# Layer norms of a transposed transformer block: the input multiplied in place by the reciprocal root, and ScalarE makes both modulated tiles and the residual from it

## The chip, the cores and the metric

The kernel runs on one core of a Trainium2 chip. The metric is device time in microseconds (us) per execution; before the change the median of three runs is 1629.13 us (1628.31 to 1630.39). Engines are named as in the profile: PE is TensorE, PEld its weight load, DVE is VectorE, ACT is ScalarE, POOL is GpSimd, SP is SyncE, which here starts the loads.

## The reference, cut to what matters

A model of two layers works on 256 tokens of a picture (`LAT`) and 256 tokens of context (`CTX`), each of width 1024. A layer is a half feed-forward (FFN), a mixer (grouped attention in layer 0, an mLSTM in layer 1) and a second half FFN. Each part is the same frame:

```python
def modulate(h, shift, scale):
    return h * (1.0 + scale) + shift

def post_norm(h, delta, g, b):
    return layer_norm(DEEPNORM_ALPHA * h + delta, g, b)

def half_ffn(h, shift, scale, gate, w_in, w_out, g, b):
    xm = modulate(h, shift, scale)
    a, u = jnp.split(xm @ w_in, 2, axis=-1)
    y = (jax.nn.silu(a) * u) @ w_out
    return post_norm(h, 0.5 * gate * y, g, b)
```

So a norm ends one part, and the modulated norm is the next part's input. In the kernel the two affine maps are folded: with z the input less its mean, and r the reciprocal root of the variance (one number per token), the next part's input is x = c·z·r + e, and what the next part's result is later added to is a·z·r + b. The coefficients a, b, c and e are one number per feature.

## The kernel before, in words

Activations lie transposed: `h` has 128 partitions, 8 chunks of 128 features, and 512 tokens in a row, tokens 0 to 255 `LAT` and 256 to 511 `CTX`. A coefficient per feature is thus one number per partition, which an ACT or DVE instruction takes from a 128x1 operand; r differs along a row, so it is spread over all partitions by a matmul with ones (L447, "the broadcast") into a PSUM tile `rb`.

Matmuls run at a fast rate with operands rounded to fp32r. To keep precision each operand is split in two tiles: a rounded one, `xh`, and the rest, `xl = x - xh`. A product is three matmuls: `xh` with the rounded weights, `xl` with the rounded weights, `xh` with the rest of the weights. Weights come from HBM in pieces of 128x1024 (`raw`, three buffers), ACT casts a piece (L225 CAST), DVE makes the rest (L230 TENSOR_TENSOR); seven finished pieces can wait.

`norm` (L443 to L546) is a generator. A table of letters at each place of use says after which matmul its next step is issued, so it is interleaved by hand with the matmuls of the FFN, of attention or of the mLSTM; its matmuls and a few statistics are pinned to that order. All other instructions go where a scheduler puts them, which at build time lists the instructions of each engine in one fixed order by its own estimates; at run time each engine works its list strictly in order. Its steps: mean (L447), eight times "subtract the mean, square" (L467 DVE, L474 ACT), variance (L447 with 128x1 results, sums by L484), the reciprocal root (L254 to L268, tiny DVE instructions), the broadcast, and eight times the **x stage** (L531 to L546), one per chunk:

- L540 DVE: x = z·c·rb, reading `rb` from PSUM
- L541 ACT: xh = x + e, rounded (bias from a 128x1 operand)
- L542 DVE: xl = (x + e) - xh
- L544 ACT, once per norm: copies `rb` to SBUF as `rs`, for the residual

The residual (L556 to L564) is put off: a list `later` holds the chunks, and the loops of the next part take two at a time: L563 DVE: z = z·a·rs, in the loops' order, and L564 ACT: z = z + b.

There are nine passes of `norm`, so 72 chunks. I name them by the time of their x stage in the profile: attention's input LAT (375 us) and CTX (400); the next FFN's LAT (555) and CTX (579); the next layer's first FFN LAT (904) and CTX (929); the mLSTM's LAT (1256) and CTX (1281, no residual is kept); the last FFN's LAT (1446), a raw norm: there the first units read z itself and are mended later (L580 to L586), and `rs` is needed for that. Residuals: 64.

In an FFN a unit is a pair of PSUM tiles (gate and up) of 128x256 for one group, 24 matmuls each. Six PSUM buffers (`mm`) hold three units; a unit's pair is free again when ACT has read the gate tile (L588, Silu) and DVE the up tile (L589). Attention: L941 to L943 are its input products, L986 and L998 to L1009 the query norm and rotation, L1036 to L1056 the softmax and the turned probabilities. L1541 and L1546, at the kernel's start, make the first part's input from the plain `h`: two ACT instructions per chunk, then a DVE subtraction.

Of the kernel before, what the change touches and what calls it, by code (L numbers as in the profile page):

```python
# [9 lines left out]
F32 = mybir.dt.float32  # L10
# [3 lines left out]
AF = mybir.ActivationFunctionType  # L14
ALU = mybir.AluOpType
# [3 lines left out]
P = 128  # L19
# [3 lines left out]
TL = 256  # L23
# [5 lines left out]
ALPHA = (2.0 * 2) ** 0.25  # L29
# [143 lines left out]
class Body:  # L173
# [23 lines left out]
    def mm(self):  # L197
        return self.t([P, 512], tag="mm", bufs=6, pool=self.pp)
# [227 lines left out]
    def pin(self, ins):  # L426

        return self.tc.keep_in_program_order(ins)
# [14 lines left out]
    def norm(self, g, coef, keep=True, nxt=True, alone=False):  # L443


        nc, V, S = self.nc, self.nc.vector, self.nc.scalar
        mm = lambda *k, **kw: self.pin(nc.tensor.matmul(*k, **kw))  # L447
        t0, t1 = g
        w = t1 - t0
        n = w // P  # L450
        raw = alone and nxt
        v = 0 if t0 == 0 else 1
# [11 lines left out]
        for d in range(ND):  # L464
            yield
            z = self.h[:, d, t0:t1]
            V.tensor_tensor(out=z, in0=z, in1=m[:, :w], op=ALU.subtract)  # L467
            if raw:
                c = coef()[1][:, v, d : d + 1]
                xh = self.xh[:, d, TL:T]  # L470
# [10 lines left out]
            else:  # L481
                a, s2 = sums[eng]
# [12 lines left out]
        x = self.small(n)  # L495
        pin = self.pin
        if most:
# [3 lines left out]
            for i in range(n):  # L501
                c = var[:, n + i : n + i + 1]
                V.tensor_scalar(c2[:, i : i + 1], c, c, -0.5, ALU.mult, ALU.mult)
            V.scalar_tensor_tensor(x, var[:, :n], 0.5 * LN_EPS, c2, ALU.add, ALU.add)
        else:
            V.tensor_scalar(x, var[:, :n], 0.5 * LN_EPS, None, ALU.add)

        r = self.rsqrt_half(x, n, pin)
        dg = self.tmp(w)
        pin(V.tensor_tensor(  # L510
            out=dg.rearrange("p (n f) -> p n f", n=n), in0=self.ident[:, None, :].broadcast_to([P, n, P]),
            in1=r[:, :, None].broadcast_to([P, n, P]), op=ALU.mult,
        ))
        if most:
# [3 lines left out]
            for d in range(ND):  # L518
                if eng[d] is not V:
                    z = self.h[:, d, t0:t1]  # L520
                    eng[d].tensor_tensor(out=z, in0=z, in1=dls, op=ALU.subtract)
        yield
        rb = self.ps()
        mm(rb[:, :w], self.ones, dg, start=True, stop=True)
        rs = self.t([P, TL], tag="rs", bufs=2) if keep and nxt else None
        if raw:
            S.copy(rs, rb[:, :w])
            dr = self.t([P, TL], tag="s1", bufs=S1B)
            V.scalar_tensor_tensor(dr, dls, -1.0, rs, ALU.mult, ALU.mult)
            self.raw_norm = rs, dr  # L530
        for d in range(ND):  # L531
            yield
            z = self.h[:, d, t0:t1]
            if most and eng[d] is V:
                V.tensor_tensor(out=z, in0=z, in1=dls, op=ALU.subtract)
            ab, c, e = coef()
            x = self.tmp(w)
            xh = self.xh[:, d, t0:t1]
            e = e[:, v, d : d + 1]
            V.scalar_tensor_tensor(x, z, c[:, v, d : d + 1], rb[:, :w], ALU.mult, ALU.mult)  # L540
            S.activation(xh, x, AF.Identity, bias=e)  # L541
            V.scalar_tensor_tensor(self.xl[:, d, t0:t1], x, e, xh.bitcast(F32), ALU.add, ALU.subtract)  # L542
            if d == 1 and rs is not None and not raw:
                S.copy(rs[:, :w], rb[:, :w])  # L544
            if keep:
                self.later.append((z, ab[:, 0, d : d + 1], ab[:, 1, d : d + 1], rs[:, :w]))  # L546

    def modulate(self, z, d, g, c, e, eng):
        t0, t1 = g
# [6 lines left out]
    def residual(self, n, pin=lambda ins: ins):  # L556

        for _ in range(min(n, len(self.later))):
            z, a, b, r = self.later.pop(0)
            if b is None:  # L560
                self.nc.scalar.activation(z, z, AF.Copy, scale=a)
            else:
                pin(self.nc.vector.scalar_tensor_tensor(z, z, a, r, ALU.mult, ALU.mult))  # L563
                self.nc.scalar.activation(z, z, AF.Identity, bias=b)  # L564


    def ffn_g(self, j, pa, pu, g, raw=False):
# [881 lines left out]
def start(b):  # L1449
# [4 lines left out]
    nc, pin = b.nc, b.pin  # L1454
    V, S = nc.vector, nc.scalar
# [73 lines left out]
    def modulated(d):  # L1529
        jobs = []  # L1530
        for v, g in enumerate((LAT, CTX)):
            z, x, xh = b.h[:, d, g[0] : g[1]], b.tmp(TL), b.xh[:, d, g[0] : g[1]]
            jobs.append((z, x, xh, ec[:, d, 0, v : v + 1], ec[:, d, 1, v : v + 1], b.xl[:, d, g[0] : g[1]]))
            b.later.append((z, ALPHA, None, None))
        for i in range(2):
            for v, (z, x, xh, e, c, _) in enumerate(jobs):
                o = x if i else xh
                if d == 0 and v and not i:
                    pin(V.tensor_scalar(o, z, c, e, ALU.mult, ALU.add))
                else:  # L1540
                    last = pin(S.activation(o, z, AF.Identity, bias=e, scale=c))  # L1541
        b.fence = {last.ins.engine: last} if d == ND - 1 else {}
        xs[d] = [(l, x, xh) for _, x, xh, _, _, l in jobs]
# [33 lines left out]
    first_by_pe()  # L1577
    cast(0)
    modulated(0)
    b.silu(pin)  # L1580
    low(ws[0][2], ws[0][0], ws[0][1])
    for d in range(ND):
# [22 lines left out]
        if n < ND:  # L1605
            modulated(n)
            low(ws[n][2], ws[n][0], ws[n][1])
# [161 lines left out]
```

## Time and profile before

| what | value |
|---|---|
| median of three runs | 1629.13 us |
| the profiled execution: its span | 1625.5 us |
| median less span | 3.6 us |
| PE busy | 1606.9 us, 99% |
| DVE busy | 1355.7 us, 83% |
| ACT busy | 749.2 us, 46% |
| POOL busy | 63.0 us, 4% |

The profile shows one execution. Its own time is the span and what lies around it (start and end); taken as 3.6 us here, the difference to the median. In rows of the timeline the first number is the start in us from the span's start, the second the time to the end of the last of the instructions grouped in the row, and "[0.68 <-ACT t L225]" says that the engine stood idle 0.68 us before it, until an ACT instruction of line 225 was done. Instructions of one engine overlap, so a group of n is shorter than n single ones.

### The profile page before, as it was taken

The page shows a single profiled execution, that of the slowest core. Times are in us where ns is not written, and L with a number is a line of the kernel's source. Part 1 is how long each engine was busy: PE and PEld are TensorE (multiplying, and loading weights), DVE is VectorE, ACT ScalarE, POOL GpSimd, SP SyncE. Part 2 cuts the span into 40 slices and gives each one's busy share as a digit, 9 for nine tenths or more (in the row PEclk, how much of TensorE's full clock was granted, in tenths as well). Part 3 has the DMA queues.
Part 4 walks back from the last instruction along what each step waited for, and adds up shares of the span by engine and source line. Part 5 has one row for each costly group of instructions (what it writes and reads, how often), then busy time and mean ns, then how long its engine had stood idle before and what let it go on. Part 6 is the DMA issues. An engine that isn't in the chain of part 4 may idle for free. (4 is left out here: it accounts for less than half of the span.)

```text
span 1625.5 us, 26587 instructions
## 1 busy us (share of the span) xinstructions
PE 1606.9 (99%) x10304; PEld 1451.7 (89%) x10304; DVE 1355.7 (83%) x2699; ACT 749.2 (46%) x1272; POOL 63.0 (4%) x77
## 2 busy tenths in 40 slices
PE   9999999999999999999999999999999999999998
PEld 7888888889988998889998998889999989999987
DVE  7899977649889879899986879699966968897687
ACT  6522132314676443316652444336652657566542
POOL 0000000001011100000000100000001000030000
PEclk9999999999999999999999999999999999999999
DMA  9687766422202447633445258713363343437552
GB/s 358 221 252 237 235 205 187 137 66 85 66 1 80 151 134 221 219 117 105 129 146 180 79 165 289 253 58 118 104 225 100 98 130 87 142 110 253 181 176 91
DMA packets 72222, 251.56 MB, mean 155 GB/s; under 512 B 7960, under 2 KB 10776, under 8 KB 72096
## 3 DMA queue, kind: packets, MB, share of 16 engines
q1 hardware_dynamic: 71520, 249.09, 47.7%
q8 instruction: 80, 1.31, 0.3%
q10 hardware_dynamic: 576, 0.79, 0.1%
q14 instruction: 46, 0.38, 0.1%
HBM read 248.79 MB, written 1.05 MB: 154 GB/s over the span
## 5 line engine op out<-in xcount | busy, mean ns | idle before, releaser
L241 PE MATMUL t<-t,t 128*128 128x256 f32 (+2 forms) x8412 | 1317.0, 318 | 6.4 <-ACT t L225 3.3
L241 PEld LDWEIGHTS t<-t,t 128*128 128x128 f32 x8412 | 1185.7, 188 | 125.4 <-ACT t L225 4.7
L225 ACT CAST t<-t 128x1024 fp32r<-128x1024 f32 (+3 forms) x521 | 428.5, 844 | 485.8 <-PE t L241 214.5
L230 DVE TENSOR_TENSOR t<-t,t 128x256 fp32r<-128x256 f32 (+2 forms) x740 | 513.8, 729 | 111.9 <-ACT t L225 107.7
L350 DVE SCALAR_TENSOR_TENSOR t<-t,t 128x1024 bf16<-128x1024 f32 x224 | 260.7, 1220 | 0.0
L588 ACT ACTIVATE t<-t 128x512 f32<-128x512 f32 (+1 forms) x71 | 34.5, 490 | 103.5 <-PE t L241 102.4
L941 PE MATMUL t<-t,t 128*128 128x256 f32 (+1 forms) x256 | 79.3, 310 | 0.0
L718 DVE SCALAR_TENSOR_TENSOR t<-t,t,t 128x256 f32<-128x256 f32 x96 | 42.7, 478 | 43.9 <-PE t L241 43.7
L943 PE MATMUL t<-t,t 128*128 128x256 f32 (+1 forms) x256 | 78.4, 306 | 0.0
L942 PE MATMUL t<-t,t 128*128 128x256 f32 (+1 forms) x256 | 78.4, 306 | 0.0
L589 DVE TENSOR_TENSOR t<-t,t 128x512 f32<-128x512 f32 (+1 forms) x71 | 39.0, 553 | 40.6 <-PE t L241 28.1
L484 POOL TENSOR_TENSOR t<-t,t 128x256 f32<-128x256 f32 x30 | 23.4, 781 | 1104.9 <-ACT t L474 1103.5
L869 PE MATMUL t<-t,t 128*128 128x512 f32 (+1 forms) x300 | 60.5, 364 | 0.0
L869 PEld LDWEIGHTS t<-t,t 128*128 128x128 f32 x300 | 51.5, 189 | 8.9
L474 ACT ACTIVATE t<-t 128x256 f32<-128x256 f32 x72 | 26.1, 412 | 65.5 <-DVE t L467 65.5
L1456 PE MATMUL t<-t,t 128*128 128x512 f32 (+2 forms) x276 | 55.6, 356 | 0.0
L1456 PEld LDWEIGHTS t<-t,t 128*128 128x128 f32 (+1 forms) x276 | 44.9, 183 | 10.9 <-issue 0.9
L942 PEld LDWEIGHTS t<-t,t 128*128 128x128 f32 x256 | 48.1, 188 | 3.0 <-DVE t L230 0.5
L941 PEld LDWEIGHTS t<-t,t 128*128 128x128 f32 x256 | 48.3, 189 | 2.7
L943 PEld LDWEIGHTS t<-t,t 128*128 128x128 f32 x256 | 48.1, 188 | 2.5
L541 ACT ACTIVATE t<-t,t 128x256 fp32r<-128x256 f32 x72 | 32.8, 503 | 30.1 <-DVE t L540 30.1
L641 DVE TENSOR_TENSOR t<-t,t 128x512 f32<-128x512 f32 x66 | 45.2, 685 | 0.4
(206 smaller groups left out, 1078.6 us busy)
## 6 DMA issues: line engine op xcount, KB each, us to landing
t<-in_ffn_in SPq DMA_DIRECT2D x168, 512.0 KB, 4.1
t<-in_ada_w SPq DMA_DIRECT2D x138, 512.0 KB, 4.4
t<-in_ffn_out SPq DMA_DIRECT2D x66, 512.0 KB, 4.5
t<-in_ffn_last SPq DMA_DIRECT2D x22, 512.0 KB, 3.5
t<-in_att_in SPq DMA_DIRECT2D x12, 512.0 KB, 3.5
t<-in_att_out SPq DMA_DIRECT2D x8, 512.0 KB, 3.6
t<-in_ml_qk SPq DMA_DIRECT2D x8, 512.0 KB, 3.6
t<-in_ml_v SPq DMA_DIRECT2D x8, 512.0 KB, 3.5
```

Of the source, the lines that this page charges most:

```text
L225: self.behind(self.nc.scalar.copy(h, x))
L230: self.behind(self.nc.vector.tensor_tensor(out=ls, in0=xs, in1=hs.bitcast(F32), op=ALU.subtract))
L241: mm = lambda *k, **kw: self.nc.tensor.matmul(*k, skip_group_check=not group, **kw)
L350: ins = nc.vector.scalar_tensor_tensor(self.tmp().bitcast(BF16), r, 1.0, self.cb[:, v, :], ALU.mult, ALU.mult, accum_out=to)
L589: V.tensor_tensor(out=sl, in0=sl, in1=pu[:, :n], op=ALU.mult)
L641: add = lambda o, x, y: V.tensor_tensor(out=o, in0=x, in1=y, op=ALU.add)
L718: V.scalar_tensor_tensor(z, y[:, gg[0] - t0 : gg[1] - t0], gate()[:, v, d : d + 1], z, ALU.mult, ALU.add)
L869: pin(nc.tensor.matmul(o, gs[g], ws[k][w][:, i : i + n], start=k == k0 and g == w == 0, stop=k == k1 - 1 and g == 1,))
L941: mm(o, self.xh[:, k, c], wh, start=k == 0, stop=False)
L942: mm(o, self.xh[:, k, c], wl, start=False, stop=False)
L943: mm(o, self.xl[:, k, c], wh, start=False, stop=k == ND - 1)
L1456: mm = lambda *k, **kw: pin(nc.tensor.matmul(*k, **kw))
```

## The change

In the x stage z is multiplied by `rb` in place (DVE, one TENSOR_TENSOR). ACT then makes xh = c·z + e and the plain x = c·z + e from it, two ACTIVATE instructions with scale and bias from 128x1 operands; DVE subtracts (TENSOR_TENSOR). Since z already holds the product with r, the residual is one ACT instruction a·z + b; its DVE part is gone, and with it `rs`, except in the raw norm, and the pin that held the residual to the loops' order.

```diff
-        rs = self.t([P, TL], tag="rs", bufs=2) if keep and nxt else None
         if raw:
+            rs = self.t([P, TL], tag="rs", bufs=1)
             S.copy(rs, rb[:, :w])
...
-            V.scalar_tensor_tensor(x, z, c[:, v, d : d + 1], rb[:, :w], ALU.mult, ALU.mult)
-            S.activation(xh, x, AF.Identity, bias=e)
-            V.scalar_tensor_tensor(self.xl[:, d, t0:t1], x, e, xh.bitcast(F32), ALU.add, ALU.subtract)
-            if d == 1 and rs is not None and not raw:
-                S.copy(rs[:, :w], rb[:, :w])
+            c = c[:, v, d : d + 1]
+            V.tensor_tensor(out=z, in0=z, in1=rb[:, :w], op=ALU.mult)
+            S.activation(xh, z, AF.Identity, bias=e, scale=c)
+            S.activation(x, z, AF.Identity, bias=e, scale=c)
+            V.tensor_tensor(out=self.xl[:, d, t0:t1], in0=x, in1=xh.bitcast(F32), op=ALU.subtract)
             if keep:
-                self.later.append((z, ab[:, 0, d : d + 1], ab[:, 1, d : d + 1], rs[:, :w]))
+                self.later.append((z, ab[:, 0, d : d + 1], ab[:, 1, d : d + 1]))
...
-                pin(self.nc.vector.scalar_tensor_tensor(z, z, a, r, ALU.mult, ALU.mult))
-                self.nc.scalar.activation(z, z, AF.Identity, bias=b)
+                self.nc.scalar.activation(z, z, AF.Identity, bias=b, scale=a)
```

New line numbers: the product in place is L541 (DVE), `xh` L542 and the plain x L543 (ACT), the subtraction L544 (DVE), the residual L563 (ACT). Lines behind it move up by one: Silu L588 becomes L587, its product L589 becomes L588.

Three places of the order, of before and of the change. First ACT's list at the end of the CTX x stage at 929 us; `t_67` is `xh`, `t_66` is `h` (z), `t_9331` in before and `t_9329` after the gate tile of the LAT unit ahead. Before:

```order
L541 ACTIVATE t_67<-t_9429,t_9030 128x256
L588 ACTIVATE t_9455<-t_9331 128x256
L541 ACTIVATE t_67<-t_9433,t_9030 128x256
L541 ACTIVATE t_67<-t_9437,t_9030 128x256
L225 CAST t_9453<-t_9455 128x256
L741 CAST t_9494<-t_67 128x256
L741 CAST t_9498<-t_67 128x256
L741 CAST t_9495<-t_68 128x256
L741 CAST t_9499<-t_68 128x256
L564 ACTIVATE t_66<-t_66,t_9023 128x256 x2
```

After the change:

```order
L542 ACTIVATE t_67<-t_66,t_9021,t_9017 128x256
L543 ACTIVATE t_9435<-t_66,t_9021,t_9017 128x256
L542 ACTIVATE t_67<-t_66,t_9021,t_9017 128x256
L543 ACTIVATE t_9440<-t_66,t_9021,t_9017 128x256
L587 ACTIVATE t_9459<-t_9329 128x256
L563 ACTIVATE t_66<-t_66,t_9014 128x256 x2
L225 CAST t_9457<-t_9459 128x256
L740 CAST t_9498<-t_67 128x256
L740 CAST t_9499<-t_68 128x256
```

The Silu (L588, now L587) that frees the gate tile stood between the stage's sixth and seventh L541; now it stands behind all sixteen activations of the stage, and the copies of `xh` and `xl` (L741, now L740) behind it and two residuals.

Second PE's list where attention's CTX products begin, at 405 us; `t_3469` is the first CTX tile in before and `t_3481` after, `t_3494` and `t_3506` the second. Rows from the sixth chunk on, before:

```order
L941 MATMUL t_3469<-t_3131,t_67 128x256
L942 MATMUL t_3469<-t_3131,t_67 128x256
L943 MATMUL t_3469<-t_3131,t_68 128x256
L941 MATMUL t_3469<-t_3131,t_67 128x256
L942 MATMUL t_3469<-t_3131,t_67 128x256
L943 MATMUL t_3469<-t_3131,t_68 128x256
L941 MATMUL t_3469<-t_3131,t_67 128x256
L942 MATMUL t_3469<-t_3131,t_67 128x256
L943 MATMUL t_3469<-t_3131,t_68 128x256
L941 MATMUL t_3494<-t_3111,t_67 128x256
```

After the change:

```order
L940 MATMUL t_3481<-t_3137,t_67 128x256
L941 MATMUL t_3481<-t_3137,t_67 128x256
L940 MATMUL t_3506<-t_3117,t_67 128x256
L941 MATMUL t_3506<-t_3117,t_67 128x256
L942 MATMUL t_3481<-t_3137,t_68 128x256
L940 MATMUL t_3481<-t_3137,t_67 128x256
L941 MATMUL t_3481<-t_3137,t_67 128x256
L942 MATMUL t_3506<-t_3117,t_68 128x256
L940 MATMUL t_3506<-t_3117,t_67 128x256
L941 MATMUL t_3506<-t_3117,t_67 128x256
L942 MATMUL t_3506<-t_3117,t_68 128x256
L940 MATMUL t_3506<-t_3117,t_67 128x256
```

Matmuls of the second tile now stand between those of the last chunks of the first, so that the last `xl` (`t_68`) of the first tile comes as the 37th matmul in place of the 24th.

Third ACT's list behind the LAT x stage at 1256 us, where the squares of the CTX norm (L474) stand; `t_13165` is in both kernels the name of a weight piece, in before as the cast result of `t_13163`, after the change as the raw piece. Before:

```order
L474 ACTIVATE t_12920<-t_66 128x256
L474 ACTIVATE t_12925<-t_66 128x256
L474 ACTIVATE t_12929<-t_66 128x256
L474 ACTIVATE t_12933<-t_66 128x256
L474 ACTIVATE t_12937<-t_66 128x256
L1209 ACTIVATE t_12961<-t_12894,t_70 128x256
L1209 ACTIVATE t_12999<-t_12966,t_70 128x256
L1213 ACTIVATE t_12851<-t_12961 128x256
L1213 ACTIVATE t_12851<-t_12999 128x256
L225 CAST t_13165<-t_13163 128x1024
L225 CAST t_13317<-t_13315 128x1024
```

After the change:

```order
L474 ACTIVATE t_12911<-t_66 128x256
L474 ACTIVATE t_12914<-t_66 128x256
L563 ACTIVATE t_66<-t_66,t_12699 128x256
L474 ACTIVATE t_12919<-t_66 128x256
L474 ACTIVATE t_12923<-t_66 128x256
L225 CAST t_13167<-t_13165 128x1024
L474 ACTIVATE t_12927<-t_66 128x256
L474 ACTIVATE t_12931<-t_66 128x256
L1208 ACTIVATE t_12955<-t_12888,t_70 128x256
```

The cast of that weight piece, which stood behind all eight squares, now stands ahead of the last two.

More of the change, by code (lines that the diff above doesn't have):

```diff
@@ L558, in residual @@
         for _ in range(min(n, len(self.later))):
-            z, a, b, r = self.later.pop(0)
+            z, a, b = self.later.pop(0)
             if b is None:
@@ L1533, in modulated @@
             jobs.append((z, x, xh, ec[:, d, 0, v : v + 1], ec[:, d, 1, v : v + 1], b.xl[:, d, g[0] : g[1]]))
-            b.later.append((z, ALPHA, None, None))
+            b.later.append((z, ALPHA, None))
         for i in range(2):
```

## The prediction

> **What bounds the kernel now.** I read the page's first part, then the busy time by stretches, then the timeline around each of the nine x stages, then the groups of instructions.
>
> The page: the span, and the busy time of each engine.
>
> ```profile
> span 1625.5 us, 26587 instructions
> PE 1606.9 (99%) x10304; PEld 1451.7 (89%) x10304; DVE 1355.7 (83%) x2699; ACT 749.2 (46%) x1272; POOL 63.0 (4%) x77
> ```
>
> PE is the bound: 18.6 us of the span are all that it idles. DVE, at 83%, limits nothing by itself. So work taken from DVE pays only where PE waits, and work given to ACT costs only where PE begins to wait. The busy time by stretches (start and end, then length, PE, PEld, DVE, ACT, POOL, clock, DMA) shows where it waits:
>
> ```profile
> 450.00:460.00 10.00, 8.16 (x49) 7.24 (x48) 8.48 (x25) 6.34 (x18) 1.01 (x1) 0.83 0.00 1
> 460.00:500.00 40.00, 35.46 (x260) 31.85 (x259) 35.66 (x85) 29.07 (x74) 8.02 (x6) 1.00 0.00 1
> 929.00:940.00 11.00, 10.97 (x94) 10.77 (x93) 8.03 (x20) 7.33 (x18) 0.00 (x0) 1.00 0.01 1
> 1446.00:1456.00 10.00, 9.28 (x75) 8.70 (x75) 10.00 (x28) 7.30 (x14) 3.42 (x4) 1.00 0.00 0
> ```
>
> Attention's scores (450 to 500 us) hold 6.4 us of idle PE, the raw norm 0.72. The CTX stage at 929 holds 0.03: there x stage and PE run side by side without slack to see, and what is to be found is how close they are.
>
> **The change part by part: the prices.** From the groups of instructions by form (busy us, mean ns of one):
>
> ```profile
> L541 ACT ACTIVATE t<-t,t 128x256 fp32r<-128x256 f32 x72 | 32.8, 503 | 30.1 <-DVE t L540 30.1
> L1541 ACT ACTIVATE t<-t,t 128x256 f32<-128x256 f32 x16 | 8.6, 587 | 0.0
> ```
>
> ```profile
> L540 DVE SCALAR_TENSOR_TENSOR t<-t,t,t 128x256 f32<-128x256 f32 x72 | 31.1, 471 | 1.4 <-PE t L447 1.4
> L563 DVE SCALAR_TENSOR_TENSOR t<-t,t,t 128x256 f32<-128x256 f32 x64 | 28.0, 478 | 0.0
> L467 DVE TENSOR_TENSOR t<-t,t 128x256 f32<-128x256 f32 x72 | 26.0, 413 | 3.2 <-PE t L447 3.2
> L1546 DVE TENSOR_TENSOR t<-t,t 128x256 fp32r<-128x256 f32 x16 | 6.3, 421 | 2.7 <-ACT t L1541 2.5
> ```
>
> L1541 is the new form itself, scale and bias both from operands: 587 ns, not L541's 503, which has a bias alone. Per chunk DVE saves 471 - 413 = 58 ns on the product and about as much on the subtraction (L1546's 421 against an instruction of L540's kind), and 478 ns with the residual: 72 x 0.11 + 64 x 0.48 = 39 us. ACT gains a whole instruction per chunk and the longer form in two others: 72 x (0.587 + 0.084) + 64 x 0.085 = 54 us, less seven copies. Busy times are not path; what an x stage takes is. Four of the new form in a row, and three of the old:
>
> ```profile
> 21.89 2.08 ACT L1541 ACTIVATE t<-t,t 128x256 fp32r<-128x256 f32 x4
> ```
>
> (2.08 - 0.587) / 3 = 0.50 us from one to the next. Sixteen in a row make an x stage 16 x 0.50 = 8.0 us long on ACT, one chunk per 1.0 us, from the first product on. Before, ACT and DVE took turns and a stage lasted some 6 to 7 us. The Trainium skill, page "ScalarE: Activation LUTs", section "Rules for kernel authors", says that multiplies and adds belong on VectorE and not on ScalarE; the same tile takes DVE 413 ns and ACT 587 here, so rule and rows agree, and the rule alone speaks for a loss without a size.
>
> **The sum, place by place.** I start ACT's chain at the first product's end, add 1.0 us per chunk and 0.5 for the subtraction behind it, and compare with the moment at which PE asks, counted in matmuls of the new order.
>
> *CTX at 929 (PE, DVE, then ACT of the timeline).*
>
> ```profile
> 928.66 1.06 PE L241 MATMUL t<-t,t 128*128 128x256 f32 x6
> ```
>
> ```profile
> 929.12 0.87 DVE L540 SCALAR_TENSOR_TENSOR t<-t,t,t 128x256 f32<-128x256 f32 x2 [0.87 <-PE t L447]
> ```
>
> ```profile
> 934.27 0.36 ACT L588 ACTIVATE t<-t 128x256 f32<-128x256 f32 x1
> ```
>
> The first xh starts at 929.6, the sixteenth activation at 929.6 + 15 x 0.497 = 937.05, and the Silu that the new list puts behind it ends at 937.05 + 0.5 + 0.36 = 937.9, where L588 was done by 934.63. The second CTX unit needs that PSUM pair: its first matmul is the 49th behind the broadcast, in both orders, due at 928.66 + 48 x 0.117 = 934.3 (0.117 us from the PE rows of the next place). Before, that was met within 0.3; now PE waits 937.9 - 934.3 = 3.6. The copies behind it (two residuals and a gate cast ahead of them) come some 0.1 late as well: **+3.7**.
>
> *Attention's CTX, 400.* The first product, four query activations that stay between the first and second chunk, PE at the first tile, and four matmuls later (0.47 / 4 = 0.117):
>
> ```profile
> 400.43 0.48 DVE L540 SCALAR_TENSOR_TENSOR t<-t,t,t 128x256 f32<-128x256 f32 x1
> ```
>
> ```profile
> 402.08 1.14 ACT L986 ACTIVATE t<-t,t 128x128 f32<-128x128 f32 x4
> ```
>
> ```profile
> 404.91 0.36 PE L941 MATMUL t<-t,t 128*128 128x256 f32 x1
> 405.11 0.28 PE L942 MATMUL t<-t,t 128*128 128x256 f32 x1
> ...
> 405.58 0.28 PE L943 MATMUL t<-t,t 128*128 128x256 f32 x1
> ```
>
> The second xh starts at 402.85, so chunk k (0 to 7) has its xl at 404.4 + (k - 1). In the new PE list the sixth chunk's xl is the 20th matmul of this stretch (due 407.1, there at 408.4), the eighth's the 37th (409.1 against 410.4). The largest gap counts, since a wait moves all that follows: **+1.3**.
>
> *FFN CTX, 579.*
>
> ```profile
> 578.21 1.04 PE L241 MATMUL t<-t,t 128*128 128x256 f32 x6
> ```
>
> ```profile
> 578.68 0.87 DVE L540 SCALAR_TENSOR_TENSOR t<-t,t,t 128x256 f32<-128x256 f32 x2 [0.54 <-PE t L447]
> ```
>
> xl k at 580.7 + k, the last at 587.7; due as the 75th matmul, 586.9. The Silu behind the sixteen frees a pair at 587.6, due as the 74th or so at 586.6: **+1.0**.
>
> *The raw norm, 1446.* ACT's first Silu, and PE's two waits in that stage before:
>
> ```profile
> 1446.72 0.51 ACT L585 ACTIVATE t<-t,t 128x256 f32<-128x256 f32 x1
> ```
>
> ```profile
> 1450.15 2.34 PE L241 MATMUL t<-t,t 128*128 128x256 f32 x18 [0.30 <-DVE t L542]
> 1452.90 0.86 PE L241 MATMUL t<-t,t 128*128 128x256 f32 x5 [0.42 <-DVE t L542]
> ```
>
> xh 0 starts at 1447.14, a gate cast stays behind the first chunk, so the second xh starts at 1448.75 and the last xl is done at 1456.35, with two of DVE's mending steps ahead of it. PE's unit begins near 1448.5; its last xl is the 46th matmul, due 1454.0. 2.35, less the 0.72 that PE idles there already: **+1.6**.
>
> *The mLSTM's two stages.* The CTX chain starts late, and a 128x1024 weight split stands between DVE's subtractions:
>
> ```profile
> 1280.75 1.65 DVE L540 SCALAR_TENSOR_TENSOR t<-t,t,t 128x256 f32<-128x256 f32 x4
> ```
>
> By the same count its last xl is at 1289.8 against 1289.2 due (+0.5). In the LAT stage the last xl is just on time, and the squares behind it come about 0.2 later into the variance. **+0.7**.
>
> *The LAT stages at 375, 555 and 904* have other matmuls for PE first; the count gives a margin of 0.2 to 3 us: **+0.1**. The weight casts that stood among the L541 and now stand behind the stage were ahead of need by several us; what hides them is that seven pieces can wait.
>
> *Attention's scores.* The gain. Eight residuals on DVE at 440 to 444, then PE's first two waits of the scores:
>
> ```profile
> 440.00 1.67 DVE L563 SCALAR_TENSOR_TENSOR t<-t,t,t 128x256 f32<-128x256 f32 x4
> ```
>
> ```profile
> 454.82 0.38 PE L241 MATMUL t<-t,t 128*128 128x256 f32 x1 [0.68 <-ACT t L225]
> 456.37 0.91 PE L241 MATMUL t<-t,t 128*128 128x256 f32 x3 [1.16 <-DVE t L230]
> ```
>
> The residuals leave this stretch on both engines, and the new PE list turns the probabilities three matmuls earlier, with ACT casting them first. I take 1.5 of the 1.84 us, between 0 and 2: **-1.5**. The other waits there hang on chains that start with PE's own products, so DVE's relief doesn't shorten them.
>
> Sum: 3.7 + 1.3 + 1.0 + 1.6 + 0.7 + 0.1 - 1.5 = +6.9. The profiled execution becomes 1632.4; with the 3.6 between its span and the median of 1629.1, the median becomes **1636.0**. The counts are each good to about 0.5 us, the raw norm to 0.8, so this case has 1632.5 to 1639.5.
>
> **The rivals.**
>
> *The cover holds.* ACT overlaps better than in L1541's rows, say 0.40 us from one to the next as a bias-only form has it:
>
> ```profile
> 931.49 1.31 ACT L541 ACTIVATE t<-t,t 128x256 fp32r<-128x256 f32 x3 [0.69 <-DVE t L540]
> ```
>
> ((1.31 - 0.50) / 2.) The stage is then 6.4 us; the Silu at 929 ends near 936.3 (+2.0), all other places are met, attention gives 1.5: 1629.1 + 0.5 = 1629.6. Against it: six groups of L1541 show 2.08, whatever lies beside them. If only part of that overlap comes, the time lies between.
>
> *Faster: DVE's relief is what attention waits for.* DVE is 85 to 89% busy through 450 to 500 us. The stage sheds 16 residuals (16 x 0.4 = 6.4 us of DVE's time), and if its chains are paced by DVE's list, most of PE's 6.4 idle us come back. Only with the x stages hidden as in the rival above does it decide: 1629.1 - 6.4 + 2.0 = 1624.7. It is decided when the waits behind 460 us shrink by more than 5. For it: the share of DVE. Against it: the residuals sat before 444, not in that stretch. In the Trainium skill, page "Perfetto Trace Analysis", section "Optimizing Scalar/DVE Operations", work may be offloaded to Scalar if DVE is saturated: that is this rival's rule; at 83% against PE's 99% the page of the profile doesn't show DVE saturated.
>
> *Slower still: a cast that waits for its load ahead of squares.* In the list of 1256 a weight cast now stands before the last two squares. Its load and cast, and PE's wait on the variance, before:
>
> ```profile
> 1273.96 3.84 SPq L210 DMA_DIRECT2D t<-in_ml_qk  x2
> ```
>
> ```profile
> 1277.43 1.05 ACT L225 CAST t<-t 128x1024 fp32r<-128x1024 f32 x1 [1.08 <-DMA t<-in_ml_qk]
> 1274.33 1.05 PE L447 MATMUL t<-t,t 128*128 128x1 f32 x8 [0.24 <-DVE t L484]
> ```
>
> The load starts when DVE has finished with an older piece, which the new DVE list does near 1268, and lands 3.5 later, at 1271.6, just when the cast's turn comes. Should it start as late as before, squares and variance slip to about 1279.4: +5 on top, 1641.
>
> **How the numbers follow.** The forecast 0.66, the cover holds 0.14, faster 0.07, the late cast 0.13. Range 1628.5 to 1640.5: it takes in the first two whole and part of the late cast. 0.2% is 3.3 us, about what a measurement of this kernel can tell from no change. Faster by more: the third case and a little of the second, 0.08. Same: the rest of the second and the forecast's low end, 0.18. Slower: 0.74.
>
> **What would show it.** L542 and L543 at 585 to 590 ns, 0.50 apart, eight pairs in 8 us; L541 and L544 on DVE at 410 to 425. Around 934 PE waits over 3 us for ACT's L587; 1 to 2 us in the stages at 405, 587 and 1450 for L544; fewer waits at 454. DVE falls by about 39 us, ACT rises by about 51, PE's busy time stays. I am wrong if PE stays above 10.8 of 11 us between 929 and 940, or if PE's idle time in the scores shrinks by several us.

## The result, and the profile after

The changed kernel takes 1637.22 us, the median of four runs (1635.57 to 1639.98), beside 1628.87 for the kernel before in the same series (1628.31 to 1630.39). The ratio is 1.0056, with an interval of 1.0042 to 1.0071: the kernel is slower by 8.35 us. The profiled execution has a span of 1635.6 us against 1625.5, which is 10.1 more. The prediction was 1636.0.

The page of the changed kernel, first its totals:

```profile
span 1635.6 us, 26578 instructions
...
PE 1611.9 (99%) x10304; PEld 1456.1 (89%) x10304; DVE 1327.2 (81%) x2635; ACT 788.3 (48%) x1337; POOL 63.4 (4%) x77
```

DVE lost 28.5 us of busy time and ACT gained 39.1, as the change says it should; PE does the same 10304 matmuls in 5.0 us more. The groups of instructions that the change made (busy us, mean ns of one, then the idle time ahead of them):

```profile
L542 ACT ACTIVATE t<-t,t,t 128x256 fp32r<-128x256 f32 x72 | 42.6, 591 | 21.1 <-DVE t L541 21.1
...
L543 ACT ACTIVATE t<-t,t,t 128x256 f32<-128x256 f32 x72 | 42.4, 588 | 0.0
...
L563 ACT ACTIVATE t<-t,t 128x256 f32<-128x256 f32 x64 | 34.9, 593 | 0.0
...
L544 DVE TENSOR_TENSOR t<-t,t 128x256 fp32r<-128x256 f32 x72 | 30.8, 428 | 11.6 <-ACT t L543 11.3
```

The two modulated tiles cost 591 and 588 ns, the rows from which the price was taken had 587. The last column of L544 is new: DVE now stands idle for ACT, 11.3 us in all, where the subtraction of before (L542) waited 1.6 us for it in all and the two engines took turns.

What PE waits for (releaser, then us in total, times, longest):

```profile
PE t L241 <- ACT t L587: 3.3, 1, 3.3
...
PE t L447 <- DVE t L484: 1.7, 1, 1.7
...
PE t L241 <- DVE t L544: 1.5, 5, 0.6
PE t L941 <- DVE t L230: 1.4, 1, 1.4
```

Three waits are new and longer than 1 us: for the Silu in the CTX stage at 929 (L587), for the variance of the latents in the norm ahead of the mLSTM (L484, a sum of squares), and for the split of a weight piece inside the mLSTM (L230). The CTX stage at 929, its first and last activations, the Silu behind them, and PE:

```profile
929.63 0.60 ACT L542 ACTIVATE t<-t,t,t 128x256 fp32r<-128x256 f32 x1 [3.68 <-DVE t L541]
...
937.03 0.58 ACT L543 ACTIVATE t<-t,t,t 128x256 f32<-128x256 f32 x1
937.52 0.36 ACT L587 ACTIVATE t<-t 128x256 f32<-128x256 f32 x1
```

```profile
937.94 7.26 PE L241 MATMUL t<-t,t 128*128 128x256 f32 x47 [3.33 <-ACT t L587]
```

Sixteen activations begin within 7.40 us, one per 0.493, the Silu ends at 937.88, and PE, which asked at 937.94 - 3.33 = 934.61, goes on at 937.94. The wait isn't all of it. The busy time by stretches around it (length, then PE, PEld, DVE, ACT, POOL, granted clock), first of before, then of after:

```profile
935.00:940.00 5.00, 5.00 (x45) 5.00 (x44) 2.34 (x6) 3.71 (x10) 0.00 (x0) 1.00 0.01 3
940.00:945.00 5.00, 5.00 (x47) 5.00 (x45) 3.85 (x11) 2.34 (x6) 0.00 (x0) 1.00 0.32 105
```

```profile
935.00:940.00 5.00, 2.06 (x10) 2.06 (x11) 2.16 (x6) 5.00 (x14) 0.00 (x0) 0.81 0.00 0
940.00:945.00 5.00, 5.00 (x39) 5.00 (x39) 0.97 (x3) 3.44 (x8) 0.00 (x0) 0.85 0.01 3
```

Behind the wait the granted clock is 0.81 and then 0.85. In shorter stretches it is plain what these means are made of, one piece of 3.41 us at half clock, all of it behind the wait:

```profile
938.08:941.49 3.41, 3.41 (x17) 3.41 (x18) 0.75 (x2) 3.30 (x9) 0.00 (x0) 0.50 0.00 0
941.49:944.90 3.41, 3.41 (x31) 3.41 (x31) 0.87 (x3) 1.96 (x4) 0.00 (x0) 1.00 0.02 5
```

PE gets 17 matmuls done in it and 31 in the next 3.41 us; fourteen fewer, at 0.113 us each, are some 1.6 us that the work behind the wait loses on top of it.

To see where the rest comes from, the program is cut at five marks that all kernels have: matmuls of L447 in the first LAT norm (373.51 us before), behind the attention block (889.97), ahead of the mLSTM (1241.88) and behind it (1425.73), and the end. The table gives the lengths between them:

| from | to | before | after | difference | forecast |
|---|---|---|---|---|---|
| LAT norm, 373 | 890: attention and the norms around it | 516.46 | 516.47 | 0.0 | +0.9 |
| 890 | 1242: LAT at 904, CTX at 929 | 351.91 | 356.40 | +4.5 | +3.7 |
| 1242 | 1426: norms at the mLSTM, mLSTM | 183.85 | 187.94 | +4.1 | +0.7 |
| 1426 | end, with the raw norm | 199.77 | 200.99 | +1.2 | +1.6 |

The missing 0.3 lies ahead of the first mark. So the 929 stage and the mLSTM's norms make 8.6 of the 10.1.

Pieces at half clock stand on both sides of this table. The first row holds one in the kernel before (456.49 to 459.91 us, 16 matmuls) and none in the changed kernel; the second and the third hold one each in the changed kernel (938.08 to 941.49, 1282.82 to 1286.23) and none before. At some 1.6 us each the three rows without them would be about +1.6, +2.9 and +2.5. And a row is good to some 0.7 us only: the second takes 352.63 in an execution of a kernel that has nothing changed there (n0 alone, below).

One of the executions behind the figures below, of the kernel with the new form in n0 alone, took 1999.82 us at a mean granted clock of 0.75; its ratio leaves it out.

### The profile page after: what moved, and what is told of

The parts are those of the page before. It is cut to its first block, busy times and chain, and to the rows that moved or that the text cites. A ratio compares the mean times of both kernels' runs of the same rounds, so it can differ in the third digit from the quotient of the medians.

```text
span 1635.6 us, 26578 instructions
## 1 busy us (share of the span) xinstructions
PE 1611.9 (99%) x10304; PEld 1456.1 (89%) x10304; DVE 1327.2 (81%) x2635; ACT 788.3 (48%) x1337; POOL 63.4 (4%) x77
## 3 DMA queue, kind: packets, MB, share of 16 engines
HBM read 248.79 MB, written 1.05 MB: 153 GB/s over the span
## 4 chain that ended last, share of the span: by engine, by line
PE 87%; DVE 7%; ACT 4%; issue 1%; DMA 0%; DVEq 0%; ACTq 0%
PE t L241 72%; PE t L1455 4%; PE t L868 4%; DVE t L230 2%; PE t L942 2%; PE t L941 2%; PE t L940 2%; ACT t L225 1%; PE t L447 1%; ACT t L543 1%; ACT t L542 1%; DVE t L541 1%; PE t L1055 0%; DVE t L467 0%; PE t L1281 0%
## 5 line engine op out<-in xcount | busy, mean ns | idle before, releaser
L241 PE MATMUL t<-t,t 128*128 128x256 f32 (+2 forms) x8412 | 1321.8, 318 | 9.0 <-ACT t L587 3.3
L241 PEld LDWEIGHTS t<-t,t 128*128 128x128 f32 x8412 | 1190.3, 189 | 128.3 <-ACT t L225 4.4
L230 DVE TENSOR_TENSOR t<-t,t 128x256 fp32r<-128x256 f32 (+2 forms) x740 | 515.0, 729 | 120.5 <-ACT t L225 114.3
L587 ACT ACTIVATE t<-t 128x512 f32<-128x512 f32 (+1 forms) x71 | 34.6, 490 | 118.3 <-PE t L241 117.1
L588 DVE TENSOR_TENSOR t<-t,t 128x512 f32<-128x512 f32 (+1 forms) x71 | 39.1, 553 | 50.9 <-PE t L241 33.1
L484 POOL TENSOR_TENSOR t<-t,t 128x256 f32<-128x256 f32 x30 | 24.1, 805 | 1111.5 <-ACT t L474 1109.9
L542 ACT ACTIVATE t<-t,t,t 128x256 fp32r<-128x256 f32 x72 | 42.6, 591 | 21.1 <-DVE t L541 21.1
L474 ACT ACTIVATE t<-t 128x256 f32<-128x256 f32 x72 | 25.6, 410 | 53.3 <-DVE t L467 53.3
```

The lines of the kernel that those rows point to most:

```text
L230: self.behind(self.nc.vector.tensor_tensor(out=ls, in0=xs, in1=hs.bitcast(F32), op=ALU.subtract))
L241: mm = lambda *k, **kw: self.nc.tensor.matmul(*k, skip_group_check=not group, **kw)
L542: S.activation(xh, z, AF.Identity, bias=e, scale=c)
```

## The experiments

Theory: a stage of sixteen activations, paced by ACT at 1.0 us a chunk, delays what stands behind it in ACT's list or needs its last subtraction, and PE pays for that at separate places. The main rivals: that the moved residuals do it, or that the loss is spread over the program. In the kernels of the experiments the lines are numbered some places higher (L241 is L243, L542 and L543 are L546 and L547, the Silu is L600, or L603 in the run with the copy; L447 is L449, L484 is L486), and a set of names says which norms use the new form; the others are as before:

```
+            if new:
+                V.tensor_tensor(out=z, in0=z, in1=rb[:, :w], op=ALU.mult)
+                S.activation(xh, z, AF.Identity, bias=e, scale=c)
+                S.activation(x, z, AF.Identity, bias=e, scale=c)
+                V.tensor_tensor(out=self.xl[:, d, t0:t1], in0=x, in1=xh.bitcast(F32), op=ALU.subtract)
+            else:
+                V.scalar_tensor_tensor(x, z, c, rb[:, :w], ALU.mult, ALU.mult)
...
```

### One part alone

The norms are n0 (ahead of the attention block), n1 (behind it), n2 (ahead of the second layer), n3 (ahead of the mLSTM) and n4 (ahead of the last feed-forward block); L and C are latents and context.

```
+NEW = ("n0L", "n1L", "n2L", "n3L", "n4L",)
```

> The new x stage and residual for the LAT norms only (five stages, 40 of the 64 residuals); the CTX norms as before. Theory (the loss is PE waiting for ACT's 1.0 us per chunk, above all in the CTX stages at 579 and 929): the places sum to -0.8 (375), +0.4 (555), 0 (904), +1.6 (1256) and +1.2 (1446), so about 2 us above the kernel before, 0.1%. Rival (the loss comes from the residuals, which now stand unpinned in ACT's list and push other work back): the LAT norms hold five eighths of them, so +5 to +6.

```
+NEW = ("n0C", "n1C", "n2C", "n3C",)
```

> The new x stage and residual for the CTX norms only (four stages, 24 residuals); the LAT norms as before. Theory: about -1 in attention, +1.3 at 579, +4.5 at 929 and +1 to +2.5 at 1281, so +6 to +7, most of the change's loss. Rival (residuals): three eighths of it, +3.

```
+NEW = ("n0L", "n0C",)
```

> The new form in attention's two input norms only (375 and 400), all else as before: the part of the change that the trace shows as a gain. Theory: the gains at the variance of 394 and in the scores stay, -1.4 to -1.8, so 0.1% faster than the kernel before. Rival (the gain in the scores hangs on the timing that other parts of the order give): within 0.5 of the kernel before.

The new form in every norm but n2C, whose x stage is the one at 929:

> The new form everywhere except in the CTX norm at 929, which is as before. Theory: the whole 4.5 us of that place come back, though PE's wait there is only 3.3, since the clock that is granted after it is lower too: about +4 above the kernel before. Rival 1 (only the wait itself comes back): +5. Rival 2 (the wait for the Silu hides a later wait, or another place takes it over): +7.

The four ran on one chip, beside 1628.66 for the kernel before:

| new form in | median | ratio, interval | over before |
|---|---|---|---|
| latents' norms | 1630.34 | 1.0011 (1.0002 to 1.0020) | +1.7 |
| context's norms | 1636.35 | 1.0049 (1.0036 to 1.0062) | +7.7 |
| n0 alone | 1628.31 | 0.9998 (0.9989 to 1.0007) | -0.4 |
| all but 929 | 1632.10 | 1.0022 (1.0013 to 1.0031) | +3.4 |

Latents and context add up (1.7 + 7.7 against 8.35 to 9), and the context has most; the rival that put +5 to +6 on the latents for their residuals falls. In the latents' run the variance at 1275 is waited for just as in the changed kernel, so that wait belongs to the latents' form:

```profile
PE t L449 <- DVE t L486: 1.7, 1, 1.7
```

The wait for the weight's split in the mLSTM isn't in the latents' trace and is 2.3 us in the context's, so it belongs to the context's form. The context's trace has the wait for the Silu too, and no half clock behind it:

```profile
939.29 20.89 PE L243 MATMUL t<-t,t 128*128 128x256 f32 x181 [3.15 <-ACT t L600]
```

The granted clock is 1.00 there from 935 to 945, and between the marks at 890 and 1242 this execution takes 355.03 us, 3.1 over before. So the wait alone costs its own length, and the half clock comes on top in some executions.

With 929 alone put back, 8.35 - 3.4 = 4.9 us return (the theory had 4 over before; the interval is 2.1 to 5.0, with the first rival's 5 at its edge), and PE no longer stops there:

```profile
935.00:940.00 5.00, 5.00 (x43) 5.00 (x44) 2.57 (x7) 3.71 (x10) 0.00 (x0) 1.00 0.02 5
```

The gain in the attention block's scores shows in the trace of the n0 run, PE being busy 54.67 of the 60 us between 440 and 500, where the kernel before has 53.63. Here are the two stretches, n0's run first, then the kernel before:

```profile
440.00:500.00 60.00, 54.67 (x399) 49.03 (x398) 50.74 (x128) 41.98 (x106) 10.95 (x7) 1.00 0.00 1
```

```profile
440.00:500.00 60.00, 53.63 (x387) 48.83 (x386) 52.04 (x133) 43.82 (x112) 10.59 (x7) 0.97 0.00 1
```

That is one microsecond less of idle time. Every trace with the new form in the context's half of n0 has it, the context's run too (54.67), and the latents' run hasn't (53.59): it belongs to that half. The 0.97 of the kernel before is the piece at half clock behind the two waits at 455; the latents' run keeps both waits and has none, so the clock isn't counted as a gain of the change. The median of the n0 run, with its interval of about 1.5 us to each side, doesn't confirm the 1.4 to 1.8 us that were expected.

### 929: how long the stage is, and what is queued behind it

Two edits at that place alone. The first shortens the second activation of each pair and leaves the order:

```
-                S.activation(x, z, AF.Identity, bias=e, scale=c)
+                if key == "n2" and t0:
+                    S.activation(x, z, AF.Copy, scale=1.0)
+                else:
+                    S.activation(x, z, AF.Identity, bias=e, scale=c)
```

> The changed kernel, with the plain tile of the context's second-layer x stage (at 929 us) alone made by a plain copy of z, so that the shift and scale are left out of that tile; the order of all instructions on every engine is otherwise that of the changed kernel. The pair of activations then takes about 0.49 + 0.32 = 0.81 us in place of 0.98, so the Silu behind all sixteen ends 8 x 0.17 = 1.4 us sooner. Theory (the stage's length on ScalarE sets the wait): TensorE's wait for the Silu falls from 3.3 to about 1.9 us, the place costs 4.5 x 1.9 / 3.3 = 2.6 instead of 4.5, time 1635.3. Rival (the place is bound by something else of the new form, the rounding subtraction or the residuals): wait and time as in the changed kernel, 1637.2.

The second keeps all sixteen activations and moves the Silu:

```
-    2: {(0, 5): 'mcccccccc', (2, 0): 'v', (2, 5): 'rxxxxxxxx'},
+    2: {(0, 5): 'mcccccccc', (2, 0): 'v', (2, 5): 'rxxxxx'},
...
                         unit_in(j, ws[j], LAT, LEADSTEP[li])
+                        if li == 2 and j == 2:
+                            self.steps("xxx")
```

> The changed kernel with the new form everywhere; only the last three of the eight steps of the x stage at 929 us are put behind the Silu of the latents' unit, so that ScalarE does the Silu behind ten of the sixteen activations (as it stood behind six of eight before). TensorE's, GpSimd's and the DMA queue's order stay word for word. Theory (what costs at 929 is the order, a Silu queued behind the activations that nobody waits for): the Silu ends at about 934.9, TensorE's wait for it falls from 3.3 to under 0.6 us, some 4 us come back, time 1633.2. Rival (the longer stage costs: the last chunks, now 0.4 to 0.7 us later still, are waited for instead): at most 1 us comes back, 1636.5 or more, and TensorE waits over 2 us for the rounding subtraction or the copies behind it.

Both ran beside 1627.06 for the kernel before. The copy: 1633.78, ratio 1.0040 (1.0027 to 1.0053), 6.7 over before. The moved Silu: 1632.90, ratio 1.0034 (1.0021 to 1.0047), 5.8 over. PE's rows and the stretch behind them, of the copy, then of the moved Silu:

```profile
937.52 8.65 PE L243 MATMUL t<-t,t 128*128 128x256 f32 x73 [1.67 <-ACT t L603]
```

```profile
935.00:940.00 5.00, 3.33 (x29) 3.13 (x28) 2.31 (x6) 5.00 (x15) 0.00 (x0) 1.00 0.00 0
```

```profile
935.05 11.15 PE L243 MATMUL t<-t,t 128*128 128x256 f32 x94 [0.40 <-ACT t L600]
```

```profile
935.00:940.00 5.00, 4.95 (x42) 4.94 (x43) 2.13 (x6) 5.00 (x12) 0.00 (x0) 1.00 0.00 0
```

With the copy the Silu starts 6.41 us after the stage's first activation, with 7.89 in the changed kernel, and the wait is 1.66 shorter. Moving the Silu out from behind six activations removed all but 0.40 of the wait, though the stage's last activation came 0.6 later than in the changed kernel. Between the marks at 890 and 1242 the copy takes 353.35 and the moved Silu 352.04, against 356.40 in the changed kernel and 351.91 before. So the stage's length costs next to nothing at 929 by itself; what costs is one Silu that frees a PSUM pair and has to queue behind activations whose results come early enough. The rival (the late chunks are waited for) falls. The medians gave back somewhat less than forecast for the moved Silu (5.8 over before instead of 4.3), with an interval, 3.4 to 7.6, that holds both.

### The plain tile on DVE

```
-                S.activation(x, z, AF.Identity, bias=e, scale=c)
+                V.tensor_scalar(x, z, c, e, ALU.mult, ALU.add)
```

> The changed kernel with the plain tile made by VectorE (z times scale plus shift, two operands per partition) instead of ScalarE: in-place product, one activation, one VectorE operation, one subtraction. VectorE gets back about 72 x 0.35 = 25 us of the 28 it lost, ScalarE loses 72 x 0.49 = 35. Theory (ScalarE's second activation is what the places pay for; VectorE's load matters little): the Silu waits for no plain tile, its wait is under 0.5 us, 4 to 5 us come back at 929, the stage's pace is 0.41 + 0.35 + 0.42 = 1.2 us per chunk and keeps the costs of the other places, time 1632.5 to 1634. Rival (VectorE's pace of 1.2 us per chunk, 9.5 us for a stage, is then the wait): TensorE waits for the subtraction by 1 to 2 us in several places, time 1636 to 1640.

Measured: 1641.04, ratio 1.0086 (1.0070 to 1.0101), 14.0 over before. The rival has the sign right and the size too small, and its mechanism only in part: it had PE wait 1 to 2 us for the subtraction in several places, and PE waits for it 1.3 us in three, the longest 0.8. What grew are waits for other work of DVE: matmuls of L243 wait for weight splits (L232) 3.1 us in five places, 0.8 in two in the changed kernel, and the means wait 2.2 us in three for a sum (L426) that isn't in the changed kernel's list at all. The changed kernel's waits in and behind the norm ahead of the mLSTM (1.7 and 1.4) are absent here. The Silu and PE's wait for it at 929:

```profile
938.81 0.36 ACT L600 ACTIVATE t<-t 128x256 f32<-128x256 f32 x1
```

```profile
939.22 6.04 PE L243 MATMUL t<-t,t 128*128 128x256 f32 x36 [2.61 <-ACT t L600]
```

The stage begins 2.0 us later than in the changed kernel (its first activation at 931.65): this execution is 1.2 behind at the mark at 890, having taken 518.51 us for 516.47 since the mark at 373, and at 917.70 PE waits 1.05 for L426. And though ACT makes only one tile per chunk here, the Silu comes 7.16 us after that first activation, 0.7 sooner than in the changed kernel and no more: ACT goes at DVE's pace, some 2.0 to 2.2 us for two chunks, and does two residuals in each of the gaps. The operation itself:

```profile
L547 DVE TENSOR_SCALAR t<-t,t,t 128x256 f32<-128x256 f32 x72 | 31.0, 459 | 0.2
```

459 ns on DVE replace 588 on ACT, and the kernel is 5 us slower by it (14.0 over before, where the changed kernel is 8 to 9 over). The Trainium skill, page "ScalarE: Activation LUTs", section "Rules for kernel authors", has add and multiply done on VectorE and not on ScalarE; by the duration of one instruction this run agrees with it, by the time of the kernel it doesn't. That DVE is the engine through which the stage's other steps go as well is the likely reason; the waits above fit it.

### The norm ahead of the mLSTM

The new form everywhere but in n3L and n3C:

> The new form everywhere but in the norm ahead of the mLSTM block (latents and context as before). The traces put +1.6 us at its latents' sums and +2.5 at its context stage and into the mLSTM. Theory: these 4.1 us come back, time 1633.1, no wait over 0.4 us for the latents' variance (1.7 in the changed kernel) and none over 0.5 for the weight's split (1.4). Rival (of the two, the wait for the weight's split is due to the residuals' order and stays): 1.6 come back, 1635.6.

Measured: 1634.10 beside 1627.06, ratio 1.0040 (1.0026 to 1.0054), 7.0 over. The median fits the rival's figure, the trace the theory's: between the marks at 1242 and 1426 this kernel takes 183.92 us, as long as before (183.85), the wait for the weight's split is absent from the list of PE's waits, and the variance has this row left:

```profile
PE t L449 <- DVE t L486: 0.2, 1, 0.2
```

The two don't agree, and the interval, from 4.2 to 8.8 us over before, holds the theory's 4.3 only at its edge. The next pair was made to decide it.

### Both repairs, and what is left

The changed kernel again, and with it the kernel that has both the old form in n3 and the moved Silu at 929:

> The new form in every norm, in the order of the changed kernel: the changed kernel once more, beside the next run on the same chip. Both theories: 8 to 9 us over the kernel before, with TensorE's waits of the changed kernel (Silu 3.3, latents' variance 1.7, weight split 1.4).

> Both repairs at once: the new form everywhere but in the norm ahead of the mLSTM block, and the Silu at 929 us ahead of the last three steps. Theory (the loss is the sum of separate places: 4.5 at 929 of which 0.4 us of wait stays, 4.1 around the mLSTM, and the rest sums to about nothing): 1629 to 1630.5 where the kernel before has 1628.9, that is 0 to 1.5 us over it, and 7 to 8 below the run before this one. Rival (part of the loss is spread over the whole program, by residuals and activations that make ScalarE late everywhere): 3 us or more over the kernel before.

On one chip, beside 1628.38: the changed kernel 1637.38, ratio 1.0055 (1.0042 to 1.0067), 9.0 over; with both repairs 1628.99, ratio 1.0001 (0.9992 to 1.0010), 0.6 over. The 8.4 us between them are what the two places were to give together, so the net loss is the sum of these two places, and the rival's loss of 3 us or more spread over the program is excluded. Smaller losses at other places remain in the traces, of the order of the gains in the attention block (next section). Of PE's waits the Silu keeps this row, and neither the variance nor the split one above 0.5:

```profile
PE t L243 <- ACT t L600: 0.4, 1, 0.4
```

The last run leaves out the new form where the traces still stood later than before:

```
+NEW = ('n0L', 'n0C', 'n1L', 'n2L', 'n2C')
```

> The run with both repairs, and the old form also in the context's norm after the attention block (579 us) and in the norm ahead of the last feed-forward block (1446 us), where the traces of all runs with the new form stand 1.0 and 1.2 us later than before. The new form is left in the norm ahead of the attention block, in the latents' norm behind it, and in the norm ahead of the second layer's first block. Theory (the places add up): the run with both repairs was 0.6 us over the kernel before in its medians and 2.0 in its spans; take away 1.0 and 1.2, and 0.2 to 1.6 us under the kernel before comes out, ratio 0.9990 to 0.9999. Rival (the attention block's shorter stretch is given back later): a ratio of 1.0 or more.

Measured: 1628.04 beside 1628.65, ratio 0.9999 (0.9990 to 1.0008). The theory's value lies in the interval, and so does no difference at all. A version that beats the kernel before by more than its noise isn't shown.

## Why the prediction was right, and where it was off

- **The mechanism and the sign.** ACT's chain of 1.0 us a chunk, and the Silu behind it that frees a PSUM pair, are as written: pitch 0.493, end of the Silu 937.88 (937.9 forecast), wait 3.33 (3.6). The rival "the cover holds" needed a pitch of 0.40. The rival in which DVE's relief brings back most of the attention block's idle time fell too: between 440 and 500 us PE's idle time went from 60 - 53.63 = 6.4 us to 5.3.
- **929 was mis-sized: +4.5 for +3.7.** The term priced the wait and not what comes behind it, the piece at half clock, some 1.6 us that the sum had nowhere ("PE's busy time stays"). It isn't paid each time: in the context's run the place cost 3.1.
- **The mLSTM was mis-sized: +4.1 for +0.7.** This is the largest miss. In the LAT stage I expected the squares 0.2 us late and found the variance 1.7 late. ACT's rows of before (its first and last squares), of after, and DVE's sum and PE behind them:

```profile
1269.00 0.42 ACT L474 ACTIVATE t<-t 128x256 f32<-128x256 f32 x1 [0.70 <-DVE t L467]
...
1271.03 1.39 ACT L474 ACTIVATE t<-t 128x256 f32<-128x256 f32 x4 [0.25 <-DVE t L467]
```

```profile
1271.47 0.60 ACT L563 ACTIVATE t<-t,t 128x256 f32<-128x256 f32 x1
...
1273.49 1.10 ACT L563 ACTIVATE t<-t,t 128x256 f32<-128x256 f32 x2
...
1274.79 1.33 ACT L474 ACTIVATE t<-t 128x256 f32<-128x256 f32 x4
1276.02 0.60 ACT L563 ACTIVATE t<-t,t 128x256 f32<-128x256 f32 x1
1276.51 0.72 ACT L474 ACTIVATE t<-t 128x256 f32<-128x256 f32 x2
1277.12 1.04 ACT L225 CAST t<-t 128x1024 fp32r<-128x1024 f32 x1
1278.07 0.73 ACT L474 ACTIVATE t<-t 128x256 f32<-128x256 f32 x2
```

```profile
1277.21 2.44 DVE L230 TENSOR_TENSOR t<-t,t 128x256 fp32r<-128x256 f32 x4
1279.58 0.41 DVE L484 TENSOR_TENSOR t<-t,t 128x256 f32<-128x256 f32 x1
```

```profile
1280.71 1.05 PE L447 MATMUL t<-t,t 128*128 128x1 f32 x8 [1.72 <-DVE t L484]
```

  Counted from the mark at 1242 (1246.68 after), the first square begins 27.1 us behind it before and 28.1 after, the last ends 30.5 and 32.1 behind it. So 1.0 of the 1.6 us is lost ahead of the squares, where ACT works off four of the moved residuals among other steps, and 0.6 among the squares, where one more residual and the weight cast stand. It is the place and the order of the rival "late cast", which was read from the list; its price wasn't, since the cast waits for no load: ACT is busy through the five microseconds from 1275 to 1280. That rival would have been +5 on top; the step that failed is the 0.2 us for the squares, which left out the residuals ahead of them and the cast and the residual that the new list already showed among them. No run moved the cast or the residuals alone. Next comes the split of a value weight in the mLSTM, on which no step of the prediction spoke:

```profile
1318.52 0.50 PE L941 MATMUL t<-t,t 128*128 128x512 f32 x1 [1.38 <-DVE t L230]
```

  and again the clock, 0.78 and 0.88 in the ten microseconds behind the variance, which is one more piece of 3.41 us at 0.50, from 1282.82 on:

```profile
1280.00:1285.00 5.00, 4.29 (x28) 4.29 (x29) 4.98 (x23) 3.04 (x6) 0.00 (x0) 0.78 0.50 130
1285.00:1290.00 5.00, 5.00 (x38) 4.95 (x38) 2.08 (x7) 1.05 (x1) 0.00 (x0) 0.88 0.84 287
```

  Why the split comes late, when the norm is over by then, no run took apart; with the old form in n3, or with the new form in the latents' norms alone, it is on time.
- **The attention block's CTX stage cost about 1.0 where +1.3 was forecast.** The list of waits shows 0.28 at the place named, and a second pause, of 0.3 us, stands in the starts of the matmuls without being listed:

```profile
406.49 0.38 PE L942 MATMUL t<-t,t 128*128 128x256 f32 x1 [0.28 <-DVE t L544]
...
407.07 0.28 PE L941 MATMUL t<-t,t 128*128 128x256 f32 x1
407.48 0.38 PE L942 MATMUL t<-t,t 128*128 128x256 f32 x1
```

  From the broadcast to the 200th matmul behind it PE takes 23.16 us before and 24.12 after. The count began with the second activation at 402.85, its time of before plus the longer form; in the trace it starts at 401.94, because the variance ahead of the stage came 0.5 earlier and the four query activations between are done sooner.
- **The scores' gain** was put at 1.5 and is 1.0 (54.69 busy of 60 us against 53.63).
- **The norm behind the attention block (+1.0)** shows no wait of L241 in the list at its place, and yet costs some 0.6: behind the broadcast 122 matmuls take 15.36 us, where 116 took 14.02 before, and six more at 0.117 are 0.7. The pauses are too short for the list. The row of the table in which these three lie holds the half clock of before as well, so its 0.0 confirms none of them; the rest of the +1.6 that it would be without that piece stays open.
- **The raw norm (+1.6)** cost some 0.9. PE's listed waits there, 0.56 and 0.24 for L544, are about what the kernel before lost to L542 in that stage (0.30 and 0.42). But from the broadcast to the 300th matmul behind it the latents' run, with the new form at this place, takes 37.47 us and the kernel before 36.53. The changed kernel has 38.34; its matmuls go at 0.118 us each behind that stage, those of the other two at 0.113, and no run shows why. So the last stretch by itself doesn't tell the cost of this norm: it is 199.86 in the latents' run with the new form here, and 201.30 in the context's run with the old.
- **The busy totals:** DVE -28.5 for -39, ACT +39 for +51. The terms multiplied counts by the duration of one instruction; neighbours overlap, an activation of 0.59 us taking 0.49 in a row, and the page counts overlapped time once.

The rows missed by +0.8, +3.4, -0.9 and -0.4, and 0.3 lies ahead of them, so that the profiled executions differ by 10.1 where the sum had 6.9. The medians differ by 8.35, since the median less the span, put at 3.6 for both, is 1.6 in the changed kernel (1637.22 - 1635.6). That took back 2.0 of the 3.2 that the sum was short, and no step forecast it: that 1636.0 is only 1.2 from the time measured is luck.

## What to carry to other kernels

When work moves to an engine with half its time free, look at who stands behind it in that engine's list: here an operation of 0.36 us, queued behind 8 us of activations whose results TensorE needed only later, cost half of the loss, and three steps moved behind it brought that back. List every instruction that the new order puts ahead of a short result that TensorE needs (a gate, a variance), and price each by its pitch. A wait of TensorE is to be priced with some extra for the clock behind it, here 0 or some 1.6 us. And count the starts of matmuls as well as the listed waits: at three places pauses too short for the list made most of the cost.

## What the runs showed of the hardware

- The granted clock fell in pieces of 3.41 us at 0.50: in each of the thirteen traces every fall between the program's first and last microseconds is one such piece, and PE did 17 matmuls in the one at 938.08 and 31 in the 3.41 us behind it.
- The length of a wait doesn't decide alone whether such a piece follows. One followed the wait of 3.33 us at 929 and the one of 1.72 at 1279; none followed the wait of 3.15 at 929 in the context's run, the one of 1.9 for the variance in the run with 929 put back, nor the one of 1.67 with the copy. What decides it no run shows. The Trainium skill, page "TensorE: Matmul & The Clock Gate", section "Why this matters for your kernels", advises to keep idle gaps between matmuls under some 3 us; the wait of 1.72 shows that less than that can cost clock, and the one of 3.15 that more needn't.
- At a granted clock of 1.00 the same kind of matmul (128x256) went at two paces: 103 of them took 11.84 us in the kernel before, from 1466.73, and 104 took 12.41 in the changed kernel, from 1476.87, which is 0.113 and 0.118 us each. No run shows why.
- DVE's operation with two operands per partition took 459 ns on average for 128x256 in fp32, not less than its subtraction of two tiles (428).
